# Context rows of the last two experts: modulation on VectorE during the last expert instead of on GpSimd behind it

## The chip, the cores and the metric

The kernel runs on one core of a Trainium2 chip. The metric is the device time of one execution in microseconds, the median of several runs. A core has a matmul engine (TensorE, "PE" in the profile, with weight loads as "PEld"), VectorE ("DVE"), ScalarE ("ACT"), GpSimd ("POOL") and the queue that issues most transfers (SyncE, "SP").

## The reference

Two layers of a transformer block work on 256 latent rows and 256 context rows of 1024 channels. Each layer is a mixer (a bidirectional recurrent part and a local attention) followed by 16 experts, of which every row takes two:

```python
y = jnp.zeros_like(t)
for e in range(N_EXPERTS):
    a = jax.nn.silu(t @ w1[e]) * (t @ w3[e])
    y = y + gate[:, e:e + 1] * (a @ w2[e])
...
x = x + mod_l[5] * h_all[:, :L]
ctx = ctx + mod_c[5] * h_all[:, L:]
```

After the experts of the first layer both kinds of rows are updated. Each kind has its own vector of 1024 factors, mod_l[5] for latent and mod_c[5] for context rows. The second layer starts with a root-mean-square norm of every row and the first projections.

## The kernel before, in words

The rows lie in `X[:, g]`, four tiles of 128 rows: g = 0, 1 are context, g = 2, 3 are latent. Weights arrive as fp32 in `raw` tiles and are split into a high and a low part: ScalarE casts (`whi`, L190) and VectorE subtracts (`wlo`, L191), for each half of a tile. Matmuls run three times, for the products of the parts.

The first layer's experts gather at most 128 rows each. `pipeline` runs them in turn: while expert e is finished, expert e+1 has its input matmuls under way. For experts 0 to 13, `done` copies the result and scatters it to rows of `yd` in memory. The last two experts skip this: their rows are brought back to row order with one-hot matrices (`oht`, made in `done` of expert 13) in matmuls of `rows` (L1526), which sum both experts in PSUM.

Around expert 14 and 15 the order in the code is this. After expert 14, `first` (L1502) keeps two copies of its result: one multiplied by the latent factors `mb5[0]` (VectorE, L1521, into the tile A), and one that is not multiplied (ScalarE, L1522, into the tile S). It reads the scattered rows of the first 14 experts back (`read`, L1534, two values for each row, into tiles `Y[g]`). GpSimd adds the two values, L1509 for latent and L1516 for context rows, in halves of 512 channels. For latent rows VectorE then multiplies by the factors (L1510) and adds to X (L1511). Before the output matmuls of expert 15, `between` starts the latent row matmuls. After expert 15, `combine` (L1538) makes the same two copies of its result (L1521, L1522), ends the latent sums, adds them to X (L1542) and starts the norm of the latent rows (`rstd_row`: squares on ScalarE L304, sums on VectorE L305 and L306, a power on GpSimd L308). Each engine takes the context rows up only after its part of that norm (`issue_after`). For each of the four halves of context rows:

```python
ps = rows(rows(self.ps(), 0, kept[0][1], g, s), 1, y, g, s)
nc.vector.tensor_tensor(z, z, ps, op=ALU.add)
nc.gpsimd.tensor_tensor(z, z, self.mb5[1][:, s], op=ALU.mult)
nc.gpsimd.tensor_tensor(self.X[:, g, s], self.X[:, g, s], z, op=ALU.add)
```

The first is L1552, the other two are L1553 and L1554. The factors come out of a small matmul and a ScalarE copy (L1225, in `mod5`, called after expert 13). The context factors `mb5[1]` lie in the buffer named S20, which is also the buffer of the tile S, so their copy comes when S has been read for the last time.

The second layer begins with `mixer_front`. Latent rows are scaled (L320 on VectorE, L321 on ScalarE), turned by TensorE (L328) and modulated into a high part `hh` (ScalarE, L339) and a low part `hl` (VectorE L340 into `hf`, then L342). The first projection (L361 to L363) works on latent columns alone and needs `hh`, `hl`, `whi` and `wlo`. Then the context rows pass through L304 to L342 in the same way, and from L400 and L401 (the gates) on, matmuls need both kinds.

The order on each engine is fixed when the program is built: a list scheduler walks over the instructions with its own model of their times and takes, among those that are ready, the one that comes first in the code.

Of the kernel before, what the change touches and what calls it, by code (L numbers as in the profile page):

```python
# [10 lines left out]
F32 = mybir.dt.float32  # L11
# [4 lines left out]
ALU = mybir.AluOpType  # L16
# [4 lines left out]
P = 128  # L21
D = 1024
# [6 lines left out]
NE = 16  # L29
# [4 lines left out]
T2, T4 = 8, 3  # L34
# [43 lines left out]
def run(gen):  # L78
    for _ in gen:
        pass  # L80
# [26 lines left out]
class Kernel:  # L107
# [1344 lines left out]
    def experts(self, l, nt, R, hd, yd, mod5):  # L1452
        nc, tc, m, m2 = self.nc, self.tc, self.m, self.m2
        ntok = nt * P
        idx, d = self.dispatch()
        XG = [self.moeA.tile([P, D], F32, name=n) for n in ("A20", "S20", "A21")]
        for x in XG:
            nc.gpsimd.memset(x, 0.0)
        scats = []
        gat = lambda e: self.gather(hd, idx[:, 0, e:e + 1], ntok, XG[e % 3]) if e < NE else None  # L1460
        gat(0)
        gat(1)
        held = self.routed, self.turned
        self.count()
        with tc.issue_after(self.routed_mm.ins), tc.issue_after(self.routed.ins):
            run(self.fill)
        self.overflow(l, nt, R, hd, yd)

        oht = R["oh"].bitcast(F32)
        Y, kept, lat, halves = {}, [], {}, [slice(0, 512), slice(512, 1024)]  # L1470

        def x_of(e):
            gat(e + 2)
            x = []
            for half in halves:
                x.append([m2.tile([P, 4, P], F32R, name=n, bufs=3) for n in ("xh", "xl")])
                self.transposed(XG[e % 3][:, half], *x[-1], slice(0, P))
            return x

        def done(e, py):  # L1480
            if e == NE - 1:
                return combine(py)
            if e == NE - 2:
                return first(py)
            y = self.work.tile([P, D], F32, name="y", tag="t4", bufs=T4)
            for half in range(2):
                nc.scalar.copy(y[:, half * 512:(half + 1) * 512], py[half])
            sc = self.scatter(yd, idx[:, 1, e:e + 1], ntok, y)
            for o in scats:
                self.tc.declare_no_dep(sc.ins, o.ins, reason="other rows")  # L1490
            scats.append(sc)
            if e == NE - 3:
                self.prefetch(6)
                with tc.issue_after(sc.ins):
                    self.prefetch(8, nc.gpsimd)
                mod5()
                for j in range(2):
                    for i in range(nt):
                        nc.vector.tensor_scalar(R["oh"][:, i, j], self.slots, float(1 + i * P),
                                                d[:, 0, NE - 2 + j:NE - 1 + j], op0=ALU.add, op1=ALU.is_equal)  # L1500

        def first(py):  # L1502

            kept.append(modulated(py, XG[(NE + 1) % 3], XG[NE % 3]))
            for g in (2, 3):
                read(g)
                for s in halves:
                    y = Y[g][:, 0, s]
                    nc.gpsimd.tensor_tensor(y, y, Y[g][:, 1, s], op=ALU.add)  # L1509
                    nc.vector.tensor_tensor(y, y, self.mb5[0][:, s], op=ALU.mult)  # L1510
                    nc.vector.tensor_tensor(self.X[:, g, s], self.X[:, g, s], y, op=ALU.add)  # L1511
            for g in (0, 1):
                read(g)
                for s in halves:
                    y = Y[g][:, 0, s]
                    nc.gpsimd.tensor_tensor(y, y, Y[g][:, 1, s], op=ALU.add)  # L1516

        def modulated(py, t, y):

            for half, s in enumerate(halves):  # L1520
                nc.vector.tensor_tensor(t[:, s], py[half], self.mb5[0][:, s], op=ALU.mult)  # L1521
                nc.scalar.copy(y[:, s], py[half])  # L1522
            return t, y

        def rows(ps, j, src, g, s):
            nc.tensor.matmul(ps, oht[:, g, j], src[:, s], start=j == 0, stop=j == 1)  # L1526
            return ps

        def between():
            for g in (2, 3):  # L1530
                for s in halves:
                    lat[g, s.start] = rows(self.ps(), 0, kept[0][0], g, s)

        def read(g):  # L1534
            Y[g] = self.rawB.tile([P, 4, 512], F32, name="raw").rearrange("p (c h) n -> p c (h n)", c=2)
            self.yread = nc.sync.dma_start(Y[g], yd.rearrange("(c i p) d -> i p c d", c=2, p=P)[g])

        def combine(py):  # L1538
            t, y = modulated(py, *(self.work.tile([P, D], F32, name=n, tag="t4", bufs=T4) for n in ("ylat", "y")))
            for g in (2, 3):  # L1540
                for s in halves:
                    nc.vector.tensor_tensor(self.X[:, g, s], self.X[:, g, s], rows(lat[g, s.start], 1, t, g, s), op=ALU.add)  # L1542
            self.lat_rows = [self.rstd_row(g) for g in (2, 3)]
            self.lat_done = self.squared, self.summed, self.powed
            with ExitStack() as behind:
                for i in self.lat_done:
                    behind.enter_context(tc.issue_after(i.ins))
                for g in (0, 1):
                    for s in halves:
                        z = Y[g][:, 0, s]  # L1550
                        ps = rows(rows(self.ps(), 0, kept[0][1], g, s), 1, y, g, s)
                        nc.vector.tensor_tensor(z, z, ps, op=ALU.add)  # L1552
                        nc.gpsimd.tensor_tensor(z, z, self.mb5[1][:, s], op=ALU.mult)  # L1553
                        nc.gpsimd.tensor_tensor(self.X[:, g, s], self.X[:, g, s], z, op=ALU.add)  # L1554
        with tc.issue_after(held[0].ins), tc.issue_after(held[1].ins):
            self.pipeline(x_of, lambda e: d[:, 1, e:e + 1], done, 1, between)

# [460 lines left out]
```

## Time and profile before

| | us |
|---|---|
| median of 3 runs | 1282.13 (1281.69 to 1283.52) |
| the profiled execution | 1284.18 |
| its span, first to last instruction | 1282.4 |
| PE busy | 1186.7 (93%) |
| VectorE busy | 733.7 (57%) |
| ScalarE busy | 586.0 (46%) |
| GpSimd busy | 222.9 (17%) |
| mean granted clock of TensorE | 0.971 |

Times in the rows are microseconds from the start of the span. Busy shares over the whole span mix stages with different limits, so the change has to be read in its own stage: from the end of expert 14 (about 686 us) to the first full stretch of the second layer (about 752 us). In a timeline row the first number is the start, the second the length from the first start to the last end of a group, and a bracket at the end gives idle time of the engine just before it and what ended it. Instructions of one engine overlap a little, so the step from one start to the next is shorter than the length of one.

### The profile page before, as it was taken

The numbers are of one execution on the slowest core, as the hardware profiler recorded it, in microseconds if no ns is written. First come the engines' busy times: TensorE is split into PE (matmuls) and PEld (weight loads), VectorE is DVE, ScalarE is ACT, GpSimd is POOL, SyncE is SP. The second block draws the span as 40 slices with busy tenths as digits, with TensorE's granted clock in tenths as the row PEclk, the third lists the DMA queues.
The fourth block names the chain that finished last, engine by engine and source line by source line (L and its number), as shares of the span: only waits on it lengthen the run. The fifth ranks groups of instructions, "written<-read, shape, count | busy, mean of one in ns | idle before, by whom it ended". The sixth has DMA issues, their size and how long they took to land. (4 is left out here: it accounts for less than half of the span.)

```text
span 1282.4 us, 16758 instructions
## 1 busy us (share of the span) xinstructions
PE 1186.7 (93%) x6133; PEld 798.6 (62%) x6133; DVE 733.7 (57%) x1284; ACT 586.0 (46%) x1001; POOL 222.9 (17%) x251
## 2 busy tenths in 40 slices
PE   4899999999977999999999799999997898989985
PEld 3588887546755788887776588986554443433322
DVE  3375454265587999998889957544458222221112
ACT  4374343255334888888776565533443110111011
POOL 2205012022043111111104524103202000000000
PEclk9999999999997999999999999999997999999998
DMA  9524115973437999999976351217966399999951
GB/s 351 214 99 177 66 59 198 352 291 122 163 148 261 358 383 376 381 380 359 355 298 237 116 177 50 99 67 239 368 250 226 142 393 412 408 405 418 384 210 55
DMA packets 55745, 322.05 MB, mean 251 GB/s; under 512 B 9212, under 2 KB 9372, under 8 KB 22361
## 3 DMA queue, kind: packets, MB, share of 16 engines
q1 hardware_dynamic: 48552, 302.77, 61.4%
q0 software_dynamic: 7088, 17.92, 4.3%
q8 instruction: 63, 1.03, 0.3%
q14 instruction: 42, 0.34, 0.1%
HBM read 313.65 MB, written 14.68 MB: 256 GB/s over the span
## 5 line engine op out<-in xcount | busy, mean ns | idle before, releaser
L191 DVE TENSOR_TENSOR wlo<-raw,whi 128x1024 fp32r<-128x1024 f32 x264 | 323.5, 1249 | 78.0 <-ACT whi L190 75.2
L190 ACT CAST whi<-raw 128x1024 fp32r<-128x1024 f32 x264 | 272.6, 1049 | 170.5 <-PE ps L1390 28.8
L1618 PE MATMUL ps<-raw,xT 128*64 128x512 f32 x424 | 114.0, 611 | 9.6 <-ACTq L1738 6.3
L1389 PE MATMUL ps<-whi,xh 128*128 128x512 f32 x256 | 102.9, 403 | 0.7 <-ACT whi L190 0.7
L1391 PE MATMUL ps<-wlo,xh 128*128 128x512 f32 x256 | 99.5, 401 | 4.2 <-DVE wlo L191 4.0
L362 PE MATMUL ps<-hl,whi 128*128 128x512 f32 (+1 forms) x256 | 97.4, 382 | 4.8 <-DVE hl L342 4.8
L1390 PE MATMUL ps<-whi,xl 128*128 128x512 f32 x256 | 101.3, 396 | 0.0
L363 PE MATMUL ps<-hh,wlo 128*128 128x512 f32 (+1 forms) x256 | 95.3, 381 | 4.4 <-DVE wlo L191 4.4
L361 PE MATMUL ps<-hh,whi 128*128 128x512 f32 (+1 forms) x256 | 94.4, 379 | 1.3 <-ACT hh L339 1.2
L1618 PEld LDWEIGHTS ps<-raw,xT 128*64 128x64 f32 x424 | 33.0, 139 | 67.2 <-issue 53.7
L379 PE MATMUL ps<-whi,hh 128*128 128x512 f32 x176 | 71.7, 408 | 0.0
L380 PE MATMUL ps<-whi,hl 128*128 128x512 f32 x176 | 70.0, 398 | 0.0
L381 PE MATMUL ps<-wlo,hh 128*128 128x512 f32 x176 | 68.6, 397 | 0.0
L1652 DVE TENSOR_TENSOR yp<-ps,X 64x512 f32<-64x512 f32 x32 | 22.0, 689 | 78.7 <-PE ps L1618 78.4
L220 PE MATMUL ps<-raw,svec 128*32 128x512 f32 (+1 forms) x416 | 61.6, 601 | 1.6 <-DMA raw<-in_ada_w_dram 1.6
L1391 PEld LDWEIGHTS ps<-wlo,xh 128*128 128x128 f32 x256 | 48.1, 188 | 22.1 <-DVE wlo L191 11.5
L1633 DVE SCALAR_TENSOR_TENSOR s<-ps,ggate,s 64x512 f32<-64x512 f32 x16 | 12.0, 749 | 86.9 <-ACT s L1629 60.1
L1618 PE MATMUL ps<-raw,aT 128*64 128x512 f32 x232 | 59.7, 594 | 1.0 <-ACT aT L1641 1.0
L362 PEld LDWEIGHTS ps<-hl,whi 128*128 128x128 f32 x256 | 51.0, 199 | 14.4 <-DVE hl L342 5.5
L363 PEld LDWEIGHTS ps<-hh,wlo 128*128 128x128 f32 x256 | 50.6, 200 | 12.8 <-DVE wlo L191 4.6
L361 PEld LDWEIGHTS ps<-hh,whi 128*128 128x128 f32 x256 | 50.0, 197 | 10.7 <-ACT hh L339 2.6
L1389 PEld LDWEIGHTS ps<-whi,xh 128*128 128x128 f32 x256 | 48.3, 189 | 11.6 <-ACT whi L190 1.9
(422 smaller groups left out, 2289.2 us busy)
## 6 DMA issues: line engine op xcount, KB each, us to landing
raw<-in_exp_w_dram SPq DMA_DIRECT2D x174, 1024.0 KB, 7.6
raw<-in_ada_w_dram SPq DMA_DIRECT2D x48, 1024.0 KB, 6.9
raw<-in_w_in_dram SPq DMA_DIRECT2D x28, 1024.0 KB, 7.1
raw<-in_w_out_dram SPq DMA_DIRECT2D x8, 1024.0 KB
whi<-in_exp_w_dram SPq DMA_DIRECT2D x16, 512.0 KB, 9.6
wlo<-in_exp_w_dram SPq DMA_DIRECT2D x16, 512.0 KB, 7.8
yd<-oz SPq DMA_DIRECT2D x8, 512.0 KB, 8.5
rpbt<-in_rpb_rows_dram POOLq DMA_DIRECT2D x16, 256.0 KB, 10.7
```

Source lines behind the costliest of these rows:

```text
L190: self.nc.scalar.copy(hi[:, :n], raw[:, k:k + n])
L191: self.nc.vector.tensor_tensor(lo[:, :n], raw[:, k:k + n], hi[:, :n].bitcast(F32), op=ALU.subtract)
L361: nc.tensor.matmul(o, hi[:, kk, s], self.hh[:, k, tok], start=k == 0, stop=False)
L362: nc.tensor.matmul(o, hi[:, kk, s], self.hl[:, k, tok], start=False, stop=False)
L363: nc.tensor.matmul(o, lo[:, kk, s], self.hh[:, k, tok], start=False, stop=k == KT - 1)
L379: nc.tensor.matmul(acc[g], self.hh[:, k, s], hi[:, kk], start=k == 0, stop=False)
L380: nc.tensor.matmul(acc[g], self.hl[:, k, s], hi[:, kk], start=False, stop=False)
L381: nc.tensor.matmul(acc[g], self.hh[:, k, s], lo[:, kk], start=False, stop=k == KT - 1)
L1389: nc.tensor.matmul(ps, xh, hi[:, kk], start=k == 0, stop=False)
L1390: nc.tensor.matmul(ps, xl, hi[:, kk], start=False, stop=False)
L1391: nc.tensor.matmul(ps, xh, lo[:, kk], start=False, stop=k == KT - 1)
L1618: nc.tensor.matmul(o[c:c + B], x, wt, start=k == 0, stop=k == n - 1, tile_position=(0, c), skip_group_check=True)
```

## The change

The context rows are treated like the latent ones. After expert 14 both kept copies are multiplied, one by the latent and one by the context factors, both on VectorE; the second goes into the buffer A20 instead of S20, and the two ScalarE copies go. The sums of the first 14 experts are multiplied and added to X on VectorE for all four tiles. After expert 15 the context copy is made on VectorE, behind the latent norm, in place of a ScalarE copy. What is left for each half of context rows is one VectorE add of PSUM to X; the two GpSimd instructions go.

```diff
         def first(py):
 
-            kept.append(modulated(py, XG[(NE + 1) % 3], XG[NE % 3]))
-            for g in (2, 3):
+            kept.extend(modulated(py, XG[(NE + 1 + r) % 3], r) for r in range(2))
+            for g in (2, 3, 0, 1):
                 read(g)
                 for s in halves:
                     y = Y[g][:, 0, s]
                     nc.gpsimd.tensor_tensor(y, y, Y[g][:, 1, s], op=ALU.add)
-                    nc.vector.tensor_tensor(y, y, self.mb5[0][:, s], op=ALU.mult)
+                    nc.vector.tensor_tensor(y, y, self.mb5[int(g < 2)][:, s], op=ALU.mult)
                     nc.vector.tensor_tensor(self.X[:, g, s], self.X[:, g, s], y, op=ALU.add)
-            for g in (0, 1):
-                read(g)
-                for s in halves:
-                    y = Y[g][:, 0, s]
-                    nc.gpsimd.tensor_tensor(y, y, Y[g][:, 1, s], op=ALU.add)
 
-        def modulated(py, t, y):
+        def modulated(py, t, r):
 
             for half, s in enumerate(halves):
-                nc.vector.tensor_tensor(t[:, s], py[half], self.mb5[0][:, s], op=ALU.mult)
-                nc.scalar.copy(y[:, s], py[half])
-            return t, y
+                nc.vector.tensor_tensor(t[:, s], py[half], self.mb5[r][:, s], op=ALU.mult)
+            return t
...
-                    lat[g, s.start] = rows(self.ps(), 0, kept[0][0], g, s)
+                    lat[g, s.start] = rows(self.ps(), 0, kept[0], g, s)
...
         def combine(py):
-            t, y = modulated(py, *(self.work.tile([P, D], F32, name=n, tag="t4", bufs=T4) for n in ("ylat", "y")))
+            new = lambda r: modulated(py, self.work.tile([P, D], F32, name="y", tag="t4", bufs=T4), r)
+            t = new(0)
...
+                y = new(1)
                 for g in (0, 1):
                     for s in halves:
-                        z = Y[g][:, 0, s]
-                        ps = rows(rows(self.ps(), 0, kept[0][1], g, s), 1, y, g, s)
-                        nc.vector.tensor_tensor(z, z, ps, op=ALU.add)
-                        nc.gpsimd.tensor_tensor(z, z, self.mb5[1][:, s], op=ALU.mult)
-                        nc.gpsimd.tensor_tensor(self.X[:, g, s], self.X[:, g, s], z, op=ALU.add)
+                        ps = rows(rows(self.ps(), 0, kept[1], g, s), 1, y, g, s)
+                        nc.vector.tensor_tensor(self.X[:, g, s], self.X[:, g, s], ps, op=ALU.add)
```

## Rows read from the trace of the kernel before

**Rows 1.** The page, span and busy time by engine (share of the span, instructions).
```profile
span 1282.4 us, 16758 instructions
...
PE 1186.7 (93%) x6133; PEld 798.6 (62%) x6133; DVE 733.7 (57%) x1284; ACT 586.0 (46%) x1001; POOL 222.9 (17%) x251
```

**Rows 2.** Windows: length, busy PE, PEld, DVE, ACT, POOL (instructions), granted clock, DMA share, GB/s.
```profile
722.00:727.00 5.00, 2.34 (x21) 2.13 (x19) 4.96 (x11) 5.00 (x11) 4.70 (x4) 1.00 0.00 0
727.00:732.00 5.00, 4.76 (x28) 4.56 (x26) 5.00 (x6) 1.83 (x6) 5.00 (x4) 0.66 0.01 2
732.00:737.00 5.00, 0.83 (x4) 0.84 (x5) 5.00 (x5) 2.29 (x5) 4.00 (x5) 0.75 0.00 0
737.00:742.00 5.00, 5.00 (x27) 5.00 (x27) 2.65 (x7) 2.23 (x3) 2.51 (x5) 0.56 0.94 339
742.00:747.00 5.00, 5.00 (x46) 5.00 (x45) 2.60 (x6) 3.48 (x7) 0.29 (x1) 1.00 1.03 311
747.00:752.00 5.00, 3.62 (x19) 2.60 (x18) 5.00 (x11) 4.67 (x10) 2.25 (x3) 1.00 0.82 310
752.00:757.00 5.00, 5.00 (x24) 4.10 (x23) 3.79 (x7) 1.23 (x3) 3.80 (x3) 1.00 0.01 3
```

**Rows 3.** Waits, 722 to 752 us: who waited for whom, total us, times, longest.
```profile
ACT junk L304 <- POOL X L1554: 4.7, 3, 2.2
...
PE ps L363 <- DVE wlo L191: 4.4, 1, 4.4
...
PE ps L362 <- DVE hl L342: 2.7, 1, 2.7
DVE wlo L396 <- ACT whi L395: 2.4, 1, 2.4
...
DVE wlo L191 <- ACT whi L190: 1.7, 1, 1.7
...
PE ps L401 <- DVE hl L342: 1.3, 1, 1.3
...
DVE xs L320 <- POOL n2q L308: 0.6, 1, 0.6
```

**Rows 4.** VectorE's timeline, 676 to 768 us: start, length, instructions, idle before.
```profile
684.08 3.60 DVE L191 TENSOR_TENSOR wlo<-raw,whi 128x1024 fp32r<-128x1024 f32 x3
...
691.47 0.69 DVE L1521 TENSOR_TENSOR A<-ps,S 128x512 f32<-128x512 f32 x1 [0.31 <-PE ps L1419]
692.31 6.20 DVE L191 TENSOR_TENSOR wlo<-raw,whi 128x1024 fp32r<-128x1024 f32 x3 [0.15 <-ACT whi L190]
...
711.09 0.68 DVE L1510 TENSOR_TENSOR raw<-raw,S 128x512 f32<-128x512 f32 x1
711.69 0.68 DVE L1511 TENSOR_TENSOR X<-X,raw 128x512 f32<-128x512 f32 x1
...
723.20 2.82 DVE L340 TENSOR_SCALAR hf<-ps,n1A,n1S 128x256 f32<-128x256 f32 x6
...
726.99 1.33 DVE L342 TENSOR_TENSOR hl<-hf,hh 128x512 fp32r<-128x512 f32 x1
...
728.70 3.00 DVE L342 TENSOR_TENSOR hl<-hf,hh 128x512 fp32r<-128x512 f32 x2
731.62 4.49 DVE L191 TENSOR_TENSOR wlo<-raw,whi 128x1024 fp32r<-128x1024 f32 x2
```

**Rows 5.** GpSimd's timeline, 676 to 768 us.
```profile
703.58 3.98 POOL L1516 TENSOR_TENSOR raw<-raw 128x512 f32<-128x512 f32 x2 [0.49 <-DMA raw<-yd]
...
722.30 5.47 POOL L1553 TENSOR_TENSOR raw<-raw,S 128x512 f32<-128x512 f32 x4 [2.29 <-ACT S L1225]
727.73 7.30 POOL L1554 TENSOR_TENSOR X<-X,raw 128x512 f32<-128x512 f32 x4
```

**Rows 6.** ScalarE's timeline, 664 to 674 us.
```profile
671.71 0.59 ACT L715 CAST xh<-ps 128x512 fp32r<-128x512 f32 x1 [1.12 <-PE ps L713]
```

**Rows 7.** Waits, 711 to 735 us.
```profile
DVE n2q L306 <- ACT junk L304: 0.9, 2, 0.5
```

## The prediction

> **What bounds the kernel now.** I start with the page [rows 1]. TensorE is busy for 93% of the span, GpSimd for 17%; taken alone that says that VectorE at 57% has room and that nothing done to GpSimd matters. Both are averages, so the second view is the windows over the passage from the experts to the second layer [rows 2]. The reader is to see three things there. VectorE is busy for 4.96, 5.00 and 5.00 of 5 us up to 737 us: here it is full. TensorE stands in 722 to 727 (5.00 - 2.34 = 2.66 us), in 732 to 737 (4.17 us) and in 747 to 752 (1.38 us), 8.45 us over the seven windows with the 0.24 of 727 to 732. [...] From 752 us on it is full at 1.00, so a microsecond taken off ahead of that point should be seen at the end.
>
> The third view, the waits [rows 3], names what ends the three stops: L342 on VectorE (2.7 us), a split L191 on VectorE (4.4 us), L342 again (1.3 us). GpSimd appears only as the one for whom ScalarE's L304 waits, 4.7 us, and no wait of TensorE names it.
>
> The fourth and fifth views, the timelines of VectorE [rows 4] and GpSimd [rows 5], show how GpSimd counts all the same. Three splits take 3.60 us at 684 us, but 6.20 us at 692 us. Between 722.30 and 735.03 us (727.73 + 7.30) GpSimd runs the eight instructions that the change removes. In that stretch L340, which reads PSUM, keeps its pace (six in 2.82 us, 0.47 each). L342 and L191, which read two tiles of SBUF, do not: 1.33 us for one L342 of a shape that takes 0.68 in L1510, 3.00 for two, 4.49 for two splits. VectorE is thus the bound, and GpSimd lengthens what VectorE does.
>
> **The change part by part.** All terms are microseconds on VectorE's own queue up to the end of the stop at 737 us, since that queue sets both long stops.
>
> Kept copy of expert 14: ScalarE's two copies become two VectorE instructions at 0.60 each (the step from one start to the next in L1510 and L1511 [rows 4]). Beside them VectorE is idle for 0.31 + 0.15 us, which covers 0.46 of 1.20: **+0.7**. Splits for expert 15 stand behind them, and TensorE waits for those. Ends: 0.7 to 1.2.
>
> The sums of the context rows: a product and an add for four halves, 8 x 0.60 = **+4.8**. GpSimd's sums for them are there at 703.58 + 3.98 = 707.56 us [rows 5], so they are ready when the latent products run. The code has them ahead of everything that comes after expert 15, and the list scheduler takes the first that is ready, so I put all eight ahead of L340. Ends: 0 (all in idle time) and 5.9 (one meets GpSimd's last sum and is stretched like the splits at 692 us, by 1.1).
>
> Kept copy of expert 15: two more instructions, behind the latent norm, 2 x 0.60 = **+1.2**. TensorE's last context matmuls now wait for them, and the turns L328 stand behind those matmuls. Ends 0 and 1.2.
>
> L1552 and the add that takes its place are four VectorE instructions of one shape each: 0. VectorE's idle time before the two L306, 0.9 us [rows 7], can take one of the context products: **-0.6**, ends 0 and -0.9.
>
> GpSimd's eight instructions go: (1.33 - 0.68) + (3.00 - 1.28) + (4.49 - 2.40) = **-4.5**, with 1.28 and 2.40 for two undisturbed ones [rows 4]. Ends: -2.1, if only the splits get their time back, and -4.5.
>
> The ScalarE copies of the context factors move from behind the context matmuls to just after expert 13, some 50 us earlier, since they no longer share a buffer. As an estimate from a ScalarE instruction of that shape they take 2 x 0.59 us, beside 1.12 us in which ScalarE waits for TensorE [rows 6]: 0, at most 1.1. They also give two of the eight PSUM buffers back, in a stretch where no wait names PSUM: 0. The reads of `yd` keep their number and their place on SP's queue, and GpSimd's queue only gets shorter.
>
> Sum on VectorE's queue: 0.7 + 4.8 + 1.2 - 0.6 - 4.5 = **+1.6**. L340 and so the first L342 come later by 0.7 + 4.8 + 1.2 - 0.6 = 6.1, so TensorE's first stop grows; but the splits behind it come only 1.6 later, so that the second stop all but vanishes, and TensorE works through from the first L362 on.
>
> Two things come back. In 737 to 742 us 27 matmuls take 5.00 us; 742 to 747 has 46 in the same time [rows 2]. At that pace 27 would take 2.9, so the lower clock after the second stop costs 2.1. Without that stop I give back half, **-1.0** (ends 0 and -2.1). Context rows reach X from VectorE before 732 us rather than from GpSimd at 735.03, so of the 1.3 us wait at L401 about half goes, **-0.7** (ends 0 and -1.3).
>
> Total: 1.6 - 1.0 - 0.7 = -0.1. The rows are of an execution of 1284.18 us (span 1282.4 and 1.78 around it), 2.05 above the median of 1282.13; I take the difference from the median: **1282.0 us**.
>
> **The rivals.**
> Faster, the work is hidden. VectorE is idle for 0.9 us before the L306 [rows 7] and 2.4, 1.7 and 0.6 us after 737 us [rows 3], 5.6 in all. If the order shifts so that all of it is used, the queue ends 6.7 - 4.5 - 5.6 = 3.4 earlier, and with the 1.0 of the clock the time is 1282.1 - 4.4 = **1277.7**. For it: ScalarE no longer waits 4.7 us for GpSimd. Against it: the three late idle stretches end with ScalarE or GpSimd, which follow TensorE there, and the code order puts the new work before them.
>
> Slower, the clock. TensorE's first stop grows from 2.66 us by up to 6.1. The profile shows 0.66, 0.75 and 0.56 after a stop of 2.66 and one of 4.17; after one of 6 or more the lower level may hold through another 27 matmuls, 2.1 us, with nothing of the two returns: 1282.1 + 1.6 + 2.1 = **1285.8**. It decides if the granted clock is still near 0.56 five microseconds after the first L362. [...]
>
> Slower, a wait in VectorE's queue. If the scheduler, by its own times, puts a context product ahead of GpSimd's sum, VectorE stands for up to the 3.98 us of the last two sums, with a split for TensorE behind it: 1282.0 + 4.0 = **1286.0**. Against it: the latent products stand far behind their sums now.
>
> Slower, nothing comes back. If L342 and L191 are long for a reason other than GpSimd, the queue only gains: 0.7 + 4.8 + 1.2 - 0.6 = +6.1, or **1288.2**. Against it: L340 keeps its pace in the same stretch, and the two that don't are those that read two tiles of SBUF. [...]
>
> That the change does not do what it says I see no room for: the context factors are free once their buffer is no longer that of the tile S.
>
> **How the numbers follow.** Chances: forecast 0.47, hidden 0.27, clock 0.19, queue 0.03, nothing back 0.04. A measurement of this kernel can tell about 0.2%, 2.6 us, from no change. The forecast lies within it, and its own range by the ends above is 1279.6 to 1284.7; hidden is faster by more, the other three slower by more: faster 0.27, same 0.47, slower 0.26. The range reaches to the prices of the hidden and the clock case, 1277.6 to 1285.9; the last two rivals lie above it.
>
> **What would show it.** Right: L1552 to L1554 gone, the L342 near 0.7 us and the splits near 1.2 each behind them, the first L362 some 4 to 6 us later, the stop at 732 to 737 us below 1 us, the context rows in X some 5 us earlier. Wrong: context products that run ahead of the output splits of expert 15 or only behind L340; L342 or L191 still stretched with GpSimd idle; a first stop that has not grown; a difference that arises after 752 us, where TensorE is full.

## The result and the profile after

| | before | after |
|---|---|---|
| median of 4 runs, us | 1282.36 (1281.69 to 1283.52) | 1291.89 (1288.64 to 1294.85) |
| ratio, 95% interval | | 1.0053 [1.0030, 1.0077] |
| the profiled execution, us | 1284.18 | 1294.85 |
| mean granted clock in it | 0.971 | 0.961 |

The changed kernel came out slower by 0.5%, 6 us above the top of the predicted range. The page, its span and engines, answers to [rows 1]:

```profile
span 1293.1 us, 16752 instructions
...
PE 1200.3 (93%) x6133; PEld 801.1 (62%) x6133; DVE 736.3 (57%) x1296; ACT 584.1 (45%) x997; POOL 210.4 (16%) x243
```

GpSimd lost its eight instructions and VectorE gained twelve; TensorE does the same 6133 matmuls and is busy for 1200.3 us with them instead of 1186.7. To find where the time went I look for the same matmuls in both timelines of TensorE, at three places: in the last expert, in the second layer's projections, and at the second layer's routing. Before:

```profile
668.43 1.19 PE L281 MATMUL ps<-mods,modselr 64*128 64x512 f32 x4
...
783.26 0.59 PE L432 MATMUL ps<-qT,rope_p 128*128 128x256 f32 x2
...
990.03 0.17 PE L1318 MATMUL ps<-r_ind,tri 128*128 128x16 bf16 x1 [5.28 <-DVE r_ind L1288]
```

After:

```profile
664.96 1.19 PE L281 MATMUL ps<-mods,modselr 64*128 64x512 f32 x4
...
780.02 0.59 PE L432 MATMUL ps<-qT,rope_p 128*128 128x256 f32 x2
...
986.78 0.17 PE L1318 MATMUL ps<-r_ind,tri 128*128 128x16 bf16 x1 [5.27 <-DVE r_ind L1288]
```

From L281 to L432, across everything the change touches, before takes 783.26 - 668.43 = 114.83 us and after 780.02 - 664.96 = 115.06: **0.2 us more**. (That after is 3.5 us ahead at L281 comes from the kernel's first 36 us, which the change leaves alone and at whose end after is 4.2 us ahead.) From L432 to L1318 it is 206.77 and 206.76. The whole loss lies behind: from L1318 to the end of the span 292.4 us before, 306.3 after. I call the first stretch the passage and the last one the last stage from here on; the last stage is the second layer's experts. The windows of exactly this stage (length, busy PE, PEld, DVE, ACT, POOL, granted clock, DMA share, GB/s), before and after:

```profile
990.03:1282.40 292.37, 254.96 (x1181) 104.29 (x1180) 67.09 (x131) 39.16 (x74) 8.18 (x16) 0.96 0.77 311
```

```profile
986.78:1293.10 306.32, 268.87 (x1181) 107.83 (x1180) 67.08 (x131) 39.11 (x74) 8.17 (x16) 0.92 0.74 297
```

TensorE is idle for 37.4 us in both. All 13.9 us are busy time of the same 1181 matmuls, at a granted clock of 0.92 instead of 0.96.

Inside the passage, VectorE's timeline after, in the stretch that answers to [rows 4]:

```profile
685.23 1.28 DVE L1516 TENSOR_TENSOR A<-ps,S 128x512 f32<-128x512 f32 x2
...
721.93 0.68 DVE L1547 TENSOR_TENSOR X<-X,ps 128x512 f32<-128x512 f32 x1
...
729.19 1.90 DVE L340 TENSOR_SCALAR hf<-ps,n1A,n1S 128x256 f32<-128x256 f32 x4 [0.75 <-ACT hh L339]
...
732.71 0.68 DVE L342 TENSOR_TENSOR hl<-hf,hh 128x512 fp32r<-128x512 f32 x1
...
736.47 2.35 DVE L191 TENSOR_TENSOR wlo<-raw,whi 128x1024 fp32r<-128x1024 f32 x2
```

L1516 writes the copies of the expert results multiplied by the factors (L1521 before); the row shown has expert 14's. L342 takes 0.68 us and two splits 2.35, where [rows 4] have 1.33 and 4.49: GpSimd runs nothing from 732.59 to 742.01 us here, and beside an idle GpSimd they take what L1510 and the splits at 684 us take in [rows 4] (0.68, and 2.40 for two), as predicted. TensorE's waits from 718 to 752 us after, against [rows 3]:

```profile
PE ps L1520 <- DVE y L1516: 3.1, 1, 3.1
PE ps L328 <- DVE hf L340: 2.5, 1, 2.5
PE ps L361 <- ACT hh L339: 1.4, 1, 1.4
```

No wait names L342 or a split any more; TensorE stands for L1516, the new product behind expert 15, instead. All three stops, 7.0 us, now lie ahead of the first L362.

The windows of the passage and of the last stage (length, TensorE busy, granted clock, DMA share, GB/s), before:

```profile
690.00:760.00 70.00, 58.40 (x261) 0.93 0.51 185
...
1000.00:1030.00 30.00, 26.76 (x140) 1.00 0.52 208
1030.00:1130.00 100.00, 92.53 (x434) 0.98 1.00 403
1130.00:1200.00 70.00, 63.98 (x306) 1.00 1.01 415
1200.00:1240.00 40.00, 36.86 (x172) 0.96 0.68 269
```

After:

```profile
690.00:760.00 70.00, 59.21 (x260) 0.90 0.46 167
...
1000.00:1030.00 30.00, 26.76 (x118) 0.89 0.55 207
1030.00:1130.00 100.00, 93.57 (x440) 0.98 0.98 401
1130.00:1200.00 70.00, 62.90 (x283) 0.95 1.01 413
1200.00:1240.00 40.00, 36.85 (x149) 0.83 0.74 277
```

In these windows of the last stage TensorE's busy share is nearly the same in both, but in three of its four windows the granted clock is lower, and from 1000 to 1030 us 118 matmuls are recorded instead of 140. The list scheduler had also put some instructions of the last stage in another order (9 of its 16 blocks differ on TensorE, 6 on VectorE, 2 on ScalarE), although the source of that stage is the same. So there are two suspects, the order (theory A) and the clock (theory B); theory C, that the passage costs it, already has these rows against it. The busy time speaks for the clock, but it doesn't say why the clock was lower.

### The profile page after: what moved, and what is told of

It reads as the page before. It is cut to its first block, busy times and chain, and to the rows that moved or that the text cites. A ratio compares the mean times of both kernels' runs of the same rounds, so it can differ in the third digit from the quotient of the medians.

```text
span 1293.1 us, 16752 instructions
## 1 busy us (share of the span) xinstructions
PE 1200.3 (93%) x6133; PEld 801.1 (62%) x6133; DVE 736.3 (57%) x1296; ACT 584.1 (45%) x997; POOL 210.4 (16%) x243
## 5 line engine op out<-in xcount | busy, mean ns | idle before, releaser
L1611 PE MATMUL ps<-raw,xT 128*64 128x512 f32 x424 | 117.8, 637 | 8.2 <-ACTq L1731 6.1
L362 PE MATMUL ps<-hl,whi 128*128 128x512 f32 (+1 forms) x256 | 94.9, 371 | 1.2 <-DVE hl L342 1.2
L1611 PE MATMUL ps<-raw,aT 128*64 128x512 f32 x232 | 63.8, 626 | 0.7 <-ACT aT L1634 0.7
L220 PE MATMUL ps<-raw,svec 128*32 128x512 f32 (+1 forms) x416 | 62.0, 605 | 2.5 <-DMA raw<-in_ada_w_dram 2.4
L1622 ACT ACTIVATE s<-ps 64x512 f32<-64x512 f32 x17 | 10.0, 591 | 100.7 <-PE ps L1611 100.7
L362 PEld LDWEIGHTS ps<-hl,whi 128*128 128x128 f32 x256 | 48.9, 191 | 10.3 <-DVE hl L342 1.7
```

Of the source, the lines that this page charges most:

```text
L362: nc.tensor.matmul(o, hi[:, kk, s], self.hl[:, k, tok], start=False, stop=False)
L1611: nc.tensor.matmul(o[c:c + B], x, wt, start=k == 0, stop=k == n - 1, tile_position=(0, c), skip_group_check=True)
```

## The experiments

All ratios are to runs of the kernel before on the same chip, in the same job. Runs of different jobs (e1 to e3; e4 to e7; e8 to e10; e11 and e12; e13 to e16) are compared only through these ratios.

**The order swapped (e1, e2, e3).** Order edges without semaphores hold the last stage's instructions on TensorE, VectorE and ScalarE in a given order (`ns` lists those of one engine in one block; the rest of the edit, with the lists, is not shown):

```diff
+            for p, q in zip(ns, ns[1:]):
+                self.tc.add_manual_dep(at[q], at[p].name, mybir.DependencyInfo(mybir.DependencyClass.NoSync, mybir.DependencyReason.DATA), reason="order of the stage")
```

> The changed kernel again, as the reference for the two swaps beside it. All theories: 1288 to 1295 us, 0.3 to 0.8% over the kernel before. The loss should again lie behind 990 us, in the second layer's experts.

> The changed kernel, with the second layer's experts (990 us to the end) held in the order that their matmuls, VectorE and ScalarE instructions had in the kernel before. Theory A (the loss is the order that the scheduler gave the second layer's experts): the loss goes, 1280 to 1284 us, ratio to before 0.998 to 1.002. Theory B (the clock: the same work, started 3 us earlier, meets the throttle at other places, whatever its order): 1288 to 1295 us, ratio 1.004 to 1.009. Theory C (the passage around 700 to 750 us itself costs it): as B, and the matmuls at 960 us would have to be late, which they were not in the first profile.

> The kernel before, with the second layer's experts held in the order that they have in the changed kernel. Theory A (order): 1288 to 1295 us, ratio to before 1.004 to 1.009, with the loss behind 990 us. Theory B (clock and phase) and theory C (the passage): 1281 to 1284 us, ratio 0.998 to 1.002.

Measured: the changed kernel again 1.0021 [0.9998, 1.0044], 1287.0 us median of 12 runs (1284.0 to 1295.0); with the order of before 1.0035 [1.0019, 1.0051]; before with the order of after 1.0029 [1.0009, 1.0049]. All theories had forecast at least 1.003 for e1, and its profile has no loss behind 990 us: the last stage takes 293.9 us there, against 306.3 in the first profile of the same program. Theory A fell for the changed kernel: undoing the order did not bring the time back (e3 alone leaves room for a part of it in the kernel before). Theory B had forecast 1281 to 1284 us for e3 and got 1288.9, so it did not hold as put either. The first 0.5% was to a good part the draw of its four runs: on this chip before itself runs from 1281.9 to 1291.8 us, and over its 29 runs a run whose mean granted clock is 0.01 higher is 7.9 us shorter (correlation -0.84).

**Control, two parts, another order (e4 to e7).**

> The kernel before against itself, nothing changed: a control on the comparison and a second profile of the same program. Theory A (the loss is an order): ratio 0.9985 to 1.0015, and the second layer's experts (980 us to the end) take the same time as in the first profile within 1.5 us. Theory B (the clock falls at holes of TensorE's work, and which holes it falls at differs from run to run of one program): the same ratio, but single runs spread over 8 to 10 us, and the stage behind 980 us differs between the two profiles by 2 to 7 us, with a lower granted clock where it is longer.

Measured: 1.0012 [0.9993, 1.0032], single runs from 1282.3 to 1291.6. In its profile the last stage takes 296.1 us, where before's first profile has 292.4: 3.7 us between two profiles of one program, 3.1 of them TensorE's busy time. Theory B's forecast; theory A's 1.5 us are exceeded.

> The kernel before, second layer's experts: in the seven even experts from 2 on, the eight matmuls that sum a pair of experts into the output (L1688) are put behind the next expert's first eight (L1618) and the four transposes (L1639); in before the first of them stands ahead, and TensorE waits 2.6 us for it at 1069, 1132 and 1243 us, 0.9 us at 1194. Theory B (clock falls at these holes, and each costs itself as well): 1273 to 1281 us, ratio 0.990 to 0.997, spread of single runs smaller than before's. Theory A (what matters is the order of VectorE and ScalarE, which stays): 1282 to 1287 us, 0.998 to 1.002. Theory D (the weights' transfers bound this stage, DMA share 1.01 from 1060 to 1200 us): no change, TensorE waits for in_exp_w_dram instead, 0.998 to 1.002.

Measured: 0.9989 [0.9971, 1.0008], outside theory B's range. But the holes did not go, so this run doesn't test what closing them is worth. ScalarE's and TensorE's timelines of e5 at the first of them:

```profile
1068.44 1.04 ACT L1696 CAST gyh<-yp 128x1024 fp32r<-128x1024 f32 x1 [4.29 <-DVE yp L1652]
...
1069.58 0.64 PE L1618 MATMUL ps<-raw,xT 128*64 128x512 f32 x1 [2.64 <-ACTq L1738]
```

L1618, which comes first in the next block here, waits 2.64 us, as L1688 waits 2.60 in before, for ScalarE's sequencer ("ACTq") at the branch that ends the block (L1738): TensorE starts 0.1 us after ScalarE's last instruction there, the cast, has ended (1068.44 + 1.04). So I had read the releaser of the 2.60 us wrongly, and e8 below follows from it.

> The changed kernel with the same order of the second layer's experts as the run before this one, instruction for instruction, so that the two differ by the change alone. Theory A and B (the change itself is worth about nothing up to 980 us; what it lost lies in the later order or clock): within 0.2% of the run before this one. Theory C (the passage at 700 to 750 us costs the time): 3 to 10 us above it.

Measured: 1.0017 [0.9997, 1.0037], 0.3% above e5. That is outside the 0.2% of theories A and B and at the lower end of theory C's 3 to 10 us, but the two intervals overlap, and in the profiles the passage differs by only 114.77 - 113.89 = 0.9 us.

> The changed kernel with the second layer's experts in the order of before (as in e2), and of the change this undone: the eight multiplications and additions of the context rows (8 x 0.6 us) go on GpSimd, at the same early place, and not on VectorE. By the terms of the prediction: VectorE's queue in the passage is 4.8 us shorter, against up to 4.5 us of slower operations beside GpSimd's, so L340 starts 0 to 5 us earlier relative to the last expert's matmuls than in e2. If a microsecond of the passage is a microsecond at the end, the matmuls at 780 us move by that too; if the passage has slack there, they stay within 1 us. The whole within 0.2% of e2 in any case.

```diff
+                    eng = nc.gpsimd if g < 2 else nc.vector
-                    nc.vector.tensor_tensor(y, y, self.mb5[int(g < 2)][:, s], op=ALU.mult)
-                    nc.vector.tensor_tensor(self.X[:, g, s], self.X[:, g, s], y, op=ALU.add)
+                    eng.tensor_tensor(y, y, self.mb5[int(g < 2)][:, s], op=ALU.mult)
+                    eng.tensor_tensor(self.X[:, g, s], self.X[:, g, s], y, op=ALU.add)
```

Measured: 1.0056 [1.0034, 1.0078], and the passage takes 786.73 - 665.04 = 121.69 us, 6.9 more than in e2. This is a miss the other way: with less on VectorE's queue the first L340 came 4.1 us later, not earlier. GpSimd's and VectorE's timelines of e7:

```profile
707.87 3.95 POOL L1512 TENSOR_TENSOR X<-X,raw 128x512 f32<-128x512 f32 x2
...
722.10 1.26 POOL L1511 TENSOR_TENSOR raw<-raw,S 128x512 f32<-128x512 f32 x1
...
723.46 0.55 POOL L308 TENSOR_TENSOR n2q<-n2q,mhalf 128x1 f32<-128x1 f32 x1
```

```profile
724.54 3.66 DVE L191 TENSOR_TENSOR wlo<-raw,whi 128x1024 fp32r<-128x1024 f32 x1
```

One add takes GpSimd some 2 us, half of the 3.95, the norm's second L308 stands behind L1511 on the same queue, and one split beside it takes 3.66 us where two take 2.35 alone. So the change's choice of VectorE for the context rows is worth 6.9 us of the passage against GpSimd at the same place. In the whole time e7 is 0.21% above e2, just outside the 0.2% that was forecast.

**Holes and slack (e8 to e10).**

> The kernel before; in the second layer's experts 3, 7 and 13 the order that expert 11 has there: of the next expert's last eight matmuls (L1618) four stand ahead of this expert's output matmuls and four behind, and ACT and DVE sum this expert's rows (L1696, L1697) ahead of the next one's activation (L1629, L1633). The trace of e5 showed that the 2.6 us hole is not the sum's place in the next block: TensorE waits at the block's end for ScalarE's last instruction, the cast at L1696, and in expert 11 only 0.9 us. Theory B' (holes at block ends, each also a place where the clock may fall): three holes shrink from 2.6 to 0.9 us, 5 us, and up to 3 us of lower clock behind them: 1276 to 1282 us, ratio 0.993 to 0.997. Theory D (transfers bound the stage): 0.999 to 1.001.

Measured: 0.9946 [0.9926, 0.9966], 1278.7 us. ScalarE and TensorE at the first of the three block ends, before:

```profile
1070.12 1.04 ACT L1696 CAST gyh<-yp 128x1024 fp32r<-128x1024 f32 x1 [4.29 <-DVE yp L1652]
...
1071.22 0.49 PE L1688 MATMUL ps<-gyh,goht 128*128 128x512 f32 x1 [2.60 <-ACTq L1738]
```

and in e8:

```profile
1071.30 1.04 ACT L1696 CAST gyh<-yp 128x1024 fp32r<-128x1024 f32 x1 [10.14 <-DVE yp L1652]
1072.37 0.59 ACT L1629 ACTIVATE s<-ps 64x512 f32<-64x512 f32 x1
...
1072.40 0.51 PE L1688 MATMUL ps<-gyh,goht 128*128 128x512 f32 x1 [0.88 <-ACT gyh L1696]
```

The last stage falls to 286.7 us, 5.7 below before's. The three holes give 3 x 1.72 = 5.2, of which 0.5 come back as three short waits just behind them and 0.6 as a longer wait for a transfer: TensorE is idle for 33.4 us instead of 37.4. The other 1.7 us are busy time. So transfers did not hold the stage at its old length, and theory D's 0.999 to 1.001 is out. Whether fewer holes also raised the clock can't be told: the 1.7 us of busy time are less than the 3.1 between two profiles of before, and most of the gain is the holes themselves.

> The changed kernel with the same second layer order as e8; the two differ by the change alone, with fewer holes behind it. If the change costs 0.4 us in the passage and nothing else (theory A, and B if the clock behind is chance), within 0.15% of e8. If it costs 3 us as in e2 and e6 (0.25%), the loss is the change's own and not that of an order behind it.

Measured: 0.9954 [0.9932, 0.9977], 0.08% above e8. Within the 0.15% of the first theory; the intervals don't exclude the second.

> The changed kernel, order of before in the second layer (as in e2), with the eight context operations on VectorE done twice in the last expert's shadow (their second time spoils the context rows' values). By the prediction, which took the passage's VectorE queue for the bound, L340 and the matmuls at 780 us come 4 to 6 us later than in e2, and so does the end (0.3 to 0.5%). If the queue has slack there (theory of slack: the context rows' operations run in time that VectorE waits through anyway), below 1.5 us at 780 us.

```diff
+                    if g < 2:
+                        nc.vector.tensor_tensor(y, y, self.mb5[1][:, s], op=ALU.mult)
+                        nc.vector.tensor_tensor(self.X[:, g, s], self.X[:, g, s], y, op=ALU.add)
```

Measured: 1.0058 [1.0034, 1.0082]; the passage 784.65 - 666.33 = 118.32 us, 3.5 above e2, and the first L340 3.4 later. Between the two forecasts: of 4.8 us put on VectorE's queue, 3.5 reach the end of the passage and 1.3 find slack. So VectorE's queue does bound the passage, as the prediction had it. The end came 0.23% later than in e2, below the 0.3 to 0.5% forecast.

**The first block (e11, e12).** The edit, on e8 and on e9:

```diff
+        mod5()
+        nc.scalar.activation(self.work.tile([P, 4], F32, name="n2q", bufs=4)[:, 0:1], G[0][4][:, 0, 0:1], AF.Silu)
         first(0, range(KT))
-        mod5()
```

> e8 and one hole less: at the start of the second layer's experts TensorE waits 2.5 us at the first block's end for ScalarE, which loads the table of its activation (1.28 us), runs it (0.59) and two copies of the last modulation (1.07) in that time. Here the two matmuls and copies of that modulation come ahead of the first expert's matmuls, and a one-column activation behind the gates' copy loads the table. Theory B' (holes are what this stage pays, and where the clock falls): the hole goes to about 0.9 us, 1.6 us less than e8 or a little more: 1275 to 1278 us, ratio 0.991 to 0.995. Theory D (transfers bound the stage): as e8, 1278 to 1280 us.

> The changed kernel with the same two edits: the pair e11 and e12 differ by the change alone. With the change, four of the seven profiles so far have the lower clock (3.4 to 6.8 us of it) right behind that hole, at 1009 to 1016 us, and of the five without the change one has (3.4 us). If the change's 2 to 4 us are this (theory B), the pair comes out within 0.1%, 1275 to 1279 us. If they are in the passage or come at any hole of the stage, e12 stays 2 to 4 us above e11 (0.15 to 0.3%).

Measured: e11 0.9954 [0.9933, 0.9976], e12 0.9930 [0.9904, 0.9956]. Both miss in size: the hole did not shrink, 2.42 and 2.39 us. ScalarE's work before it did, but in e12 the wait (us, times, longest) became TensorE's own sequencer at the branch:

```profile
PE ps L1611 <- PEq L1732: 2.4, 1, 2.4
```

And yet e12 has the lowest ratio of the study, and here the change is 0.24% *faster* than its counterpart: the sign turned. The same edit that leaves the hole as it was moved the kernel before by +0.08% and the changed one by -0.24%. A fixed cost of the change would not do that; but the intervals overlap, so the turn may be noise.

**Work added ahead of the last stage (e13 to e16).** Order as in before, plus repeats of one matmul at 948 us, where TensorE is full (five in e13 and e15, ten in e14 and e16):

```diff
+                if l and not k and g == tiles[0] and not hasattr(self, "repeated"):
+                    self.repeated = True
+                    for _ in range(5):
+                        nc.tensor.matmul(acc, mh[:, k, s], hi[:, kk], start=True, stop=True)
```

> The kernel before, its order of the second layer's experts held, with the first matmul of the second layer's output projection (948 us, where TensorE is full) issued five times more: 5 x 0.23 = 1.15 us of TensorE work, and no other difference. Theory F (costs add up): 1.1 us over before, 0.0 to 0.15%. Theory B (the clock behind depends on when the stage starts): the matmuls at 960 us come about 1.1 us later and the end by something else, between 3 us earlier and 5 us later.

> The same with ten repeats, 2.3 us. Theory F: 2.3 us over before, 0.1 to 0.25%. Theory B: not in proportion to e13; a spread of the whole between -3 and +5 us over before.

> The changed kernel with the order of before (e2: 1290.4 us median) and five repeats, 1.15 us. Theory F: 1.15 us over e2, 1291 to 1292 us, ratio to before about 1.0045. Theory B: the change put the stage where the clock falls most often, and any delay can move it away: e15 or e16 comes out below e2 by 2 us or more, although it does more work.

> The changed kernel with the order of before and ten repeats, 2.3 us. Theory F: 2.3 us over e2, 1292 to 1293.5 us, ratio about 1.0055. Theory B: as e15.

Measured: e13 0.9986 [0.9970, 1.0003], e14 1.0007 [0.9993, 1.0020], e15 1.0007 [0.9986, 1.0028], e16 0.9999 [0.9979, 1.0018]. The changed kernel with 1.15 and 2.3 us of added work is 0.28 and 0.36% *below* the same kernel without it (e2, 1.0035). For the changed kernel that is theory B's forecast, and both intervals lie below theory F's 1.0045 and 1.0055, though e2's own interval, from 1.0019, takes away a part of that gap. For the kernel before, theory F is not excluded: e14's +0.07% lies in its interval, and e13's interval reaches the 0.0%. The windows show three draws: TensorE from 1010 to 1015 us, and the matmuls behind the first block's hole, in e2, in e15 and in e13:

```profile
1010.00:1015.00 5.00, 4.95 (x12) 0.50 0.96 400
...
1010.05 6.67 PE L1611 MATMUL ps<-raw,xT 128*64 128x512 f32 x16 [2.52 <-ACTq L1731]
```

```profile
1010.00:1015.00 5.00, 4.67 (x24) 1.00 0.94 382
...
1010.33 3.65 PE L1615 MATMUL ps<-raw,xT 128*64 128x512 f32 x16 [2.52 <-ACTq L1735]
```

```profile
1010.00:1015.00 5.00, 5.00 (x14) 0.50 1.01 424
...
1009.33 6.58 PE L1622 MATMUL ps<-raw,xT 128*64 128x512 f32 x16 [2.52 <-ACTq L1742]
```

The hole is 2.52 us in all three. Behind it, sixteen matmuls take 3.65 us in e15, 6.67 in e2 and 6.58 in e13: from 1010 to 1015 us the granted clock is 0.50 in e2 and e13 and 1.00 in e15. So the drop behind the first hole is in e2 and e13 and not in e15 and before. That the 1.15 us of added work did this is not shown. The last stage begins at 990.03 us in before and at 987.91 in e4, the same program, but at 986.41 in e13, earlier in spite of the added work; between before and after the first 36 us alone make 4.2 us, of which 3.5 are left at L281. And e15's profile is of the fastest of its twelve runs (1282.4 to 1291.8 us).

All profiles, one per run; passage and last stage measured as above, "begins" is the start of L1318 (L1322 in e13 to e16), the clock is that of the window of 1000 to 1030 us:

| kernel (last stage's order) | ratio | passage | begins | last stage | clock |
|---|---|---|---|---|---|
| before (before) | 1 | 114.8 | 990.03 | 292.4 | 1.00 |
| e4, before again (before) | 1.0012 | 115.3 | 987.91 | 296.1 | 1.00 |
| e13, before + 1.15 (before) | 0.9986 | 113.9 | 986.41 | 297.6 | 0.89 |
| e14, before + 2.3 (before) | 1.0007 | 115.1 | 989.19 | 298.0 | 0.89 |
| e2, after (before) | 1.0035 | 114.8 | 986.94 | 298.1 | 0.89 |
| e15, after + 1.15 (before) | 1.0007 | 115.0 | 987.84 | 292.8 | 1.00 |
| e16, after + 2.3 (before) | 0.9999 | 114.7 | 989.88 | 295.4 | 1.00 |
| e7, context on GpSimd (before) | 1.0056 | 121.7 | 993.25 | 297.1 | 0.89 |
| e10, context twice (before) | 1.0058 | 118.3 | 991.41 | 297.6 | 0.94 |
| e3, before (after) | 1.0029 | 115.0 | 986.85 | 299.0 | 1.00 |
| after, first profile (after) | 1.0053 | 115.1 | 986.78 | 306.3 | 0.89 |
| e1, after (after) | 1.0021 | 116.2 | 989.27 | 293.9 | 1.00 |
| e5, before (late sums) | 0.9989 | 113.9 | 986.07 | 294.6 | 0.94 |
| e6, after (late sums) | 1.0017 | 114.8 | 987.62 | 293.4 | 1.00 |
| e8, before (split) | 0.9946 | 115.5 | 990.26 | 286.7 | 1.00 |
| e9, after (split) | 0.9954 | 114.8 | 988.56 | 293.1 | 0.89 |
| e11, before (split, early) | 0.9954 | 115.2 | 989.36 | 290.1 | 1.00 |
| e12, after (split, early) | 0.9930 | 115.0 | 987.35 | 289.5 | 1.00 |

Three readings. With the change as it is (after, e1, e2, e6, e9, e12, e15, e16) the passage takes 115.0 us in the mean, without it 114.8 (before, e3, e4, e5, e8, e11, e13, e14), each spreading by 1.5 or so: 0.2 us. Among the nine profiles with the order of before, the last stage takes 292.4, 296.1, 292.8 and 295.4 us where the clock is 1.00 in that window, and 297.1 to 298.1 where it is 0.89 or 0.94, with kernels of both kinds on both sides: 294.2 and 297.7 in the mean, 3.5 us apart. And the lower clock in that window doesn't go with the change: three of the eight profiles with it have one (after, e2, e9) and three of the eight without it (e5, e13, e14). By the time at which the stage begins the profiles fall into groups: lower at 986.07 to 986.94 (all but e3), not at 987.35 to 987.91, lower at 988.56 and 989.19, not at 989.27 to 990.26, lower at 991.41 and 993.25. That order was found afterwards in eighteen profiles; no run tested it. One profile shows one draw of a kernel; the ratios are over 4 to 12 runs of it.

## Why the prediction was right about the passage and wrong about the time

*VectorE is the bound, and GpSimd lengthens what it does.* Right. L342 and the splits came back to 0.68 and 2.35 us; 4.8 us more on VectorE moved the passage by 3.5 (e10); the same work on GpSimd cost 6.9 (e7). The rival that nothing comes back is out.

*Sum of the passage, -0.1 us.* Right: 0.2 in the first pair of profiles and in the mean of sixteen. But its parts were off, and that they cancel is luck. The first L340 came 64.23 us behind L281 instead of 54.77, 9.5 later where 6.1 were forecast, and the first L362 69.12 instead of 58.24, 10.9 later and not 4 to 6: TensorE now waits 3.1 us for the product L1516 behind expert 15, a wait the sum had priced at the instructions' 1.2. Behind the first L362 10.7 us came back, where 4.5 + 1.0 + 0.7 = 6.2 were forecast: no second long stop, and L342 at full pace. The context rows were in X 4.8 us earlier (61.8 us behind L281 instead of 66.6), as the signs had it.

*Clock in the passage, -1.0.* Not seen. The granted clock from 690 to 760 us is 0.93 before and 0.90 after. It did fall behind the 3.1 us stop, ahead of the first L362 (windows of after, columns as in [rows 2]):

```profile
720.00:725.00 5.00, 5.00 (x7) 2.02 (x6) 3.72 (x8) 2.47 (x6) 1.34 (x4) 0.50 0.00 0
...
739.00:744.00 5.00, 5.00 (x44) 5.00 (x43) 5.00 (x7) 3.03 (x6) 1.99 (x3) 1.00 0.86 313
```

Five microseconds after the first L362 (734.08) it is at 1.00, so the clock rival, 1285.8, is out by its own sign. It put the slower clock into the passage; the loss came from the clock in another stage.

*"From 752 us on it is full at 1.00, so a microsecond taken off ahead of that point should be seen at the end."* This is the step that failed. It holds up to 990 us: the 206.8 us from L432 to L1318 are the same to 0.01. It does not hold from there on. The last stage has holes of 0.3 to 2.6 us at its block ends, and the clock falls behind some and not others: in before it is 0.50 from 1072.6 to 1074.6 us, behind the 2.60 us hole that ends at 1071.22, and 1.00 from 1135 to 1139 us, behind the 2.60 us hole that ends at 1135.08. The same 1181 matmuls keep TensorE busy for 254.96 us in before's first profile, for 268.87 in after's and for 255.68 in e1's, which is the same program as after, at a granted clock of 0.96, 0.92 and 0.96. So one kernel can end in 306.3 or 293.9 us of last stage, 12.4 us apart, more than any term of the sum. What decides behind which holes the clock falls stays open. The sum had no term for that. Nor is the prediction's own range, 1279.6 to 1284.7, what its ends give: added up they are -8.1 to +7.3, or 1274.0 to 1289.4, and 1279.6 to 1284.7 is 0.2% on either side of the median. The sign named as wrong, a difference that arises after 752 us, is what came.

*The 0.2% that a measurement can tell.* Too fine for three or four runs: before against itself gave 1.0012 with an interval of 0.4% in width, and before's single runs on one chip spread over 10 us, 0.8% of its time. The base of the forecast, 1282.13 us from three runs, was itself a low draw: in the five later jobs the median of the kernel before is 1285.2 to 1287.3. The two profiled executions differ from their start: the L220 behind the first projections begin at 32.08 us in after and at 36.28 in before, where fourteen matmuls ahead of them take 0.43 us a step instead of 0.23, some 2.8 us.

What the change costs by itself: nothing in the passage that can be told from zero. In whole times e1 and e2 stand at 1.0021 and 1.0035 of before, e6 at 1.0017 against 0.9989 of e5, e9 at 0.9954 against 0.9946 of e8, e12 at 0.9930 against 0.9954 of e11, e15 at 1.0007 against 0.9986 of e13, and e16 at 0.9999 against 1.0007 of e14. Five are slower and two faster, by 0.12% in the mean of the seven, from -0.24 to +0.35%. A cost of a few tenths of a per cent is neither shown nor excluded. The five slower ones also have the lower mean granted clock over their runs (e2 0.965 against 0.970, e15 0.968 against 0.972), so what they lose goes with the clock; whether the change brings that about stays open.

A better kernel came out of it: the order of e8 alone is 0.9946 [0.9926, 0.9966] of before. With the change and the early modulation (e12) it is 0.9930 [0.9904, 0.9956], which can't be told from e8.

## What to carry to other kernels

Before saying that a microsecond saved is seen at the end, look at every stage behind it: here one with idle holes, at a granted clock under 1.00 (0.92 to 0.96 in before, after and e1), differed by 3.7 us (before and e4) and by 12.4 us (after and e1) between two executions of one program, and so hides a change of one. Set TensorE's busy and idle time over the same matmuls side by side: here the idle time was equal, and the busy time pointed at the clock. Compare the same matmuls in two traces at the borders of the stages to find where a difference arises, and profile the old kernel twice before explaining one of half a per cent. Holes at block ends are worth closing for themselves (three of 2.60 us cut to 0.88 in e8, and TensorE was idle for 33.4 us instead of 37.4): look at which engine's last instruction holds the branch.

## What was not expected of the hardware

Of one program, two profiles differ in one stage by 3.7 us (before and e4) or by 12.4 (after and e1). With the same hole of 2.52 us ahead of them, the same sixteen matmuls take 3.65 or 6.58 us. And at the branch that ends a block the trace names different releasers for TensorE's wait: 2.64 us for ScalarE's sequencer, though the block's first matmul doesn't need the cast that ScalarE ran last (e5), and 2.39 us for its own sequencer where ScalarE is early (e12).
